# Running sums of squares on VectorE instead of GpSimd in a one-layer streaming encoder

## The chip, the cores and the metric

The kernel runs on one core of one Trainium2 chip. A core has five engines with instruction queues of their own, each worked off in order: TensorE (PE in the profile, its weight loads PEld), VectorE (DVE), ScalarE (ACT), GpSimd (POOL) and SyncE (SP, which here issues DMAs). They meet through semaphores. The metric is the device time of one execution in microseconds (us), the median of several runs.

## The reference

One layer of an encoder is applied to two groups of rows with the same weights: 1024 prompt rows and 32 sample rows of width 1024. Cut to what matters here:

```python
def rms_norm(x, g):
    y = xf * lax.rsqrt(jnp.mean(xf * xf, axis=-1, keepdims=True) + EPS)
    return (y * g.astype(jnp.float32)).astype(x.dtype)

h = rms_norm(x, g_mix)
z = h @ w_in                     # q, k, v, conv, gates
a = attn_core(q, k, v) @ w_attn_out
bo = (cb * conv) @ w_conv_out
x = x + (jax.nn.sigmoid(ga) * a + jax.nn.sigmoid(gb) * bo) @ w_mix_out      # "mixed" rows
hc = rms_norm(x, g_cross)
x = x + co @ w_co                # co: attention of hc @ w_cq into 256 memory tokens; "crossed" rows
hm = rms_norm(x, g_mlp)
x = x + jnp.square(jax.nn.relu(hm @ w_up)) @ w_down                         # "last" rows
y = rms_norm(x, norm_final_g)
```

All is float32. Each `rms_norm` needs the mean of the squares of a row over its 1024 features.

## The kernel before, in words

The rows lie along the free axis of a tile and the features along the 128 partitions, so that x is 8 tiles (f = 0 to 7) for each of three chunks of rows (c = 0, 1, 2 with 384, 384 and 288 columns). A product in full precision is made of three matrix products on TensorE (`gemm`, L176 to L178; `do_co`, L1293 to L1295; `part`, L1706 to L1708): operands are split into a rounded high part (ScalarE, L120, or L150 for a kept weight) and a rest (VectorE, L121). A weight of 128x1024 is fetched by SyncE, split into `wh` and `wl`, and taken by TensorE up to three weights later.

The sum over features has two steps. Along f, the squares of the tiles are added up, column by column, into a piece of the tile `xacc`; this is `square_acc`. For f = 0 the square is written straight into `xacc`, for f > 0 into a temporary tile `ct` and then added. Then `stats_col` (L207) lets TensorE add up the 128 partitions into `pq`, and VectorE and ScalarE make the factor 1/sqrt (L209 to L215), which `stats_row` spreads over a tile R (L223 to L226). `ct` has six buffers, used in turn by many steps; a buffer is free again when its last reader is done.

`square_acc` is called in three stages, for each chunk:
- `do_mix` (mixed rows): VectorE adds the product in the accumulator to the row (L1154, into a tile of `Ga` or `Gb`), `gain_split` splits it for the next product (L256 on ScalarE, L257 on VectorE), and the square of f = 0 to 6 is made by GpSimd (L249), that of f = 7 by ScalarE (L251).
- `do_co` (crossed rows): TensorE makes the products of two tiles f side by side in two of the three accumulators; VectorE adds each to the row (L1298), ScalarE squares it (L251).
- `to_x1` with `squares_of` (last rows): VectorE adds the last product (L1696), ScalarE squares it (L251). For chunk 2 the last square is not added; `last_row` gives it to TensorE as a second operand (L1752).

Chunk c's cross attention stands beside chunk c+1's mixing in the program (`beside`), so that crossed rows of one chunk and mixed rows of the next share a stretch of time. GpSimd also adds in `do_conv_out` (L1140), squares in `up_part` (L1356), and makes sums of weights (L881 to L884); a kernel-wide scheduler fixes the order of instructions in each queue from durations that it assumes, except for those pinned by hand. At the end `final` and `final_last` scale the rows and store them (L1741, L1788, L1790).

Of the kernel before, what the change touches and what calls it, by code (L numbers as in the profile page):

```python
# [13 lines left out]
ALU = mybir.AluOpType  # L14
# [24 lines left out]
def hybrid_step(ctx: ExitStack, tc: tile.TileContext, io):  # L39
    nc = tc.nc  # L40
    act, dve, pool_e, pe, sp = nc.scalar, nc.vector, nc.gpsimd, nc.tensor, nc.sync
# [54 lines left out]
    def tmp(n, dt=F32):  # L96
        return tp.tile([P, n], dt, tag="ct", bufs=NCT, name=nm("ct"))
# [144 lines left out]
    def square_acc(x, f, c, on_pool=False):  # L242
        n = CH[c][1]
        if f == 0:
            accs[c] = [xacc[0][:, CH[c][0] : CH[c][0] + n]]
        acc = accs[c][0]
        sq = tmp(n) if f else acc
        if on_pool:
            pool_e.tensor_tensor(sq, x, x, op=ALU.mult)  # L249
        else:  # L250
            act.activation(sq, x, AF.Square)  # L251
        if f:
            pool_e.tensor_tensor(acc, acc, sq, op=ALU.add)  # L253

    def scaled_split(hi, lo, x, g):
        act.mul(hi, x, col(g))  # L256
# [889 lines left out]
    def do_mix(c, f):  # L1146
        def fn(w):
            n = CH[c][1]
            xt = cr.tile([P, n], F32, tag="xt", bufs=3, name=nm("xt"))
            sp.dma_start(xt, io[f"x{c}"][:, f])  # L1150
            a = acc_tile([P, n])
            gemm(a, w, mg[c])
            x = gate_slot(c, f)
            dve.tensor_add(x, a, xt)  # L1154
            x1[c][f] = x
            xc[c][f] = gain_split(x, G_CROSS + f, c)
            square_acc(x, f, c, on_pool=f < NF - 1)

        return fn
# [122 lines left out]
    def do_co(c, half):  # L1282
        def fn(w):
            n = CH[c][1]
            wh, wl = w
            fs = range(4 * half, 4 * half + 4)
            for f in fs:
                if f % 2 == 0:
                    two = [acc_tile([P, n]) for _ in range(2)]
                    for k, g in ((k, g) for k in range(2) for g in range(2)):  # L1290
                        s = slice((((f + g) % 4) * 2 + k) * P, (((f + g) % 4) * 2 + k) * P + P)
                        hi, lo = co[c][k]
                        pe.matmul(two[g], wh[:, s], hi, start=(k == 0), stop=False)  # L1293
                        pe.matmul(two[g], wh[:, s], lo, start=False, stop=False)
                        pe.matmul(two[g], wl[:, s], hi, start=False, stop=(k == 1))  # L1295
                a = two[f % 2]
                x = x1[c][f]
                dve.tensor_add(x, a, x)  # L1298
                if half == 0 and c == 2:
                    xm[c][f] = gain_split(x, G_MLP + f, c)  # L1300
                square_acc(x, f, c)
            if half == 1 and c == 2:
                for f in fs:
                    xm[c][f] = gain_split(x1[c][f], G_MLP + f, c)

        return fn
# [377 lines left out]
    def squares_of(c, x):  # L1684

        if c == 2 and done[c] == NF - 1:
            sq = tmp(CH[c][1])
            act.activation(sq, x, AF.Square)
            accs[c].append(sq)
        else:  # L1690
            square_acc(x, done[c], c)
        done[c] += 1
# [283 lines left out]
```

## Time and profile before

| | |
|---|---|
| median of 3 runs | 1769.81 us (1769.12 to 1770.55) |
| the profiled execution's own time | 1767.74 us |
| its span (first to last instruction) | 1766.0 us |
| granted TensorE clock, mean | 0.997 |
| busy: PE, DVE, ACT, POOL | 1733.7, 1213.3, 846.1, 657.9 us |
| the adds of `square_acc` (L253) | 62 on POOL, 78.0 us |

Rows of the profile name an engine, a line of the kernel (L253), the tile written and those read (`xacc<-xacc,ct`), and partitions x elements. A group row has the busy time in us and the mean of one in ns, then the idle time of the engine just before, with what ended it. A timeline row has its start and its length in us, and in brackets the idle time before it. In a row of a chain there are a start, a length, and what ran.

### The profile page before, as it was taken

How to read it: one execution, taken by the hardware profiler on the slowest of the kernel's cores; microseconds unless marked ns; L12 is line 12 of the kernel's file. 1: busy time of each engine (PE TensorE's matmuls, PEld its weight loads, DVE VectorE, ACT ScalarE, POOL GpSimd, SP SyncE). 2: the span in 40 equal slices, each digit the busy share in tenths (PEclk: the TensorE clock that was granted, in tenths of full speed). 3: DMA queues.
4: the chain of work that ended last, by engine and by line, in shares of the span. 5: the costliest groups of instructions: out<-in, count | busy, mean ns of one | idle time of the engine just before them, and what ended most of it. 6: DMA issues, size and time to landing. Idle time of an engine off the chain costs nothing.

```text
span 1766.0 us, 30039 instructions
## 1 busy us (share of the span) xinstructions
PE 1733.7 (98%) x11008; PEld 1711.6 (97%) x11008; DVE 1213.3 (69%) x2130; ACT 846.1 (48%) x1625; POOL 657.9 (37%) x702
## 2 busy tenths in 40 slices
PE   8999999999999999999999999999999999999997
PEld 8999999999999999999999999999999999999997
DVE  6768888777887767367576877666666675445665
ACT  8667767852232245144465755642222353432553
POOL 2246675643744534402324241375544300100111
PEclk9999999999999999999999999999999999999998
DMA  5413434442322527789766767744443497544674
GB/s 183 146 58 106 141 114 147 139 153 98 132 86 96 177 102 263 261 255 320 259 218 208 242 219 240 253 166 155 130 139 124 149 316 221 176 152 141 230 240 134
DMA packets 178115, 313.01 MB, mean 177 GB/s; under 512 B 18192, under 2 KB 137776, under 8 KB 177840
## 3 DMA queue, kind: packets, MB, share of 16 engines
q1 hardware_dynamic: 168320, 276.97, 47.2%
q0 software_dynamic: 9216, 33.56, 5.4%
q8 instruction: 86, 1.41, 0.3%
q10 hardware_dynamic: 432, 0.58, 0.1%
q14 instruction: 61, 0.50, 0.1%
HBM read 233.23 MB, written 77.81 MB: 176 GB/s over the span
## 4 chain that ended last, share of the span: by engine, by line
PE 72%; DMA 9%; DVE 6%; ACT 5%; issue 3%; POOL 2%; SPq 1%; POOLq 0%; DVEq 0%; ACTq 0%
PE acc L176 7%; PE acc L178 7%; PE acc L177 7%; PE acc L892 7%; PE acc L894 7%; PE acc L893 7%; PE acc L1707 5%; PE acc L1706 5%; PE acc L1708 5%; PE pa L177 3%; PE pa L178 3%; PE pa L176 3%; DVE wl L121 2%; ACT wh L120 1%; PE pt L589 1%
## 5 line engine op out<-in xcount | busy, mean ns | idle before, releaser
L120 ACT CAST wh<-wr 128x1024 fp32r<-128x1024 f32 (+1 forms) x224 | 234.1, 1045 | 311.4 <-PE acc L1707 77.1
L121 DVE TENSOR_TENSOR wl<-wr,wh 128x1024 fp32r<-128x1024 f32 (+1 forms) x224 | 307.3, 1372 | 93.2 <-ACT wh L120 91.7
L176 PE MATMUL acc<-Y,wh 128*128 128x384 f32 (+1 forms) x624 | 201.9, 324 | 2.6 <-DVE ct L1081 1.5
L178 PE MATMUL acc<-Y,wl 128*128 128x384 f32 (+1 forms) x624 | 201.6, 323 | 0.3 <-DVE wl L121 0.3
L177 PE MATMUL acc<-Y,wh 128*128 128x384 f32 (+1 forms) x624 | 201.6, 324 | 0.0
L253 POOL TENSOR_TENSOR xacc<-xacc,ct 128x384 f32<-128x384 f32 (+1 forms) x62 | 78.0, 1257 | 322.2 <-ACT ct L251 319.8
L176 PE MATMUL acc<-X,wh 128*128 128x384 f32 (+1 forms) x528 | 172.6, 327 | 1.2 <-ACT wh L120 1.2
L177 PE MATMUL acc<-X,wh 128*128 128x384 f32 (+1 forms) x528 | 171.8, 325 | 0.9 <-DVE X L257 0.9
L178 PE MATMUL acc<-X,wl 128*128 128x384 f32 (+1 forms) x528 | 171.0, 324 | 0.0
L176 PEld LDWEIGHTS acc<-Y,wh 128*128 128x128 f32 x624 | 117.0, 188 | 3.9 <-DVE ct L1081 1.9
L178 PEld LDWEIGHTS acc<-Y,wl 128*128 128x128 f32 x624 | 117.2, 188 | 0.6 <-DVE wl L121 0.6
L177 PEld LDWEIGHTS acc<-Y,wh 128*128 128x128 f32 x624 | 117.1, 188 | 0.0
L579 POOL TENSOR_SCALAR S<-S,rec 128x256 f32<-128x256 f32 (+1 forms) x96 | 93.3, 984 | 62.1 <-DVE rec L576 61.9
L1706 PE MATMUL acc<-Y,wh 128*128 128x384 f32 (+1 forms) x352 | 113.1, 321 | 0.2 <-ACT Y L120 0.2
L1707 PE MATMUL acc<-Y,wh 128*128 128x384 f32 (+1 forms) x352 | 113.1, 321 | 0.1
L1708 PE MATMUL acc<-Y,wl 128*128 128x384 f32 (+1 forms) x352 | 112.9, 321 | 0.0
L120 ACT CAST wh<-s 128x1024 fp32r<-128x1024 f32 x54 | 56.6, 1051 | 105.9 <-PE acc L893 72.3
L177 PEld LDWEIGHTS acc<-X,wh 128*128 128x128 f32 x528 | 100.0, 189 | 2.9 <-DVE X L257 1.8
L176 PEld LDWEIGHTS acc<-X,wh 128*128 128x128 f32 x528 | 99.8, 189 | 2.2 <-ACT wh L120 1.4
L178 PEld LDWEIGHTS acc<-X,wl 128*128 128x128 f32 x528 | 99.8, 189 | 1.0 <-DVE wl L121 0.2
L121 DVE TENSOR_TENSOR Y<-ct,Y 128x384 fp32r<-128x384 f32 (+1 forms) x128 | 68.9, 570 | 28.7 <-ACT Y L120 28.5
L120 ACT CAST Y<-ct 128x384 fp32r<-128x384 f32 (+1 forms) x128 | 59.2, 486 | 60.0 <-DMA ct<-bc_d 14.8
(405 smaller groups left out, 5360.3 us busy)
## 6 DMA issues: line engine op xcount, KB each, us to landing
wr<-in_w_in SPq DMA_DIRECT2D x55, 512.0 KB, 3.6
wr<-in_w_up SPq DMA_DIRECT2D x48, 512.0 KB, 3.8
wr<-in_w_down SPq DMA_DIRECT2D x32, 512.0 KB, 4.0
wr<-wsum_d SPq DMA_DIRECT2D x32, 512.0 KB, 3.5
wl<-wl_d SPq DMA_DIRECT2D x28, 512.0 KB, 4.8
wr<-in_w_conv_out SPq DMA_DIRECT2D x24, 512.0 KB, 4.5
wr<-in_w_mix SPq DMA_DIRECT2D x24, 512.0 KB, 4.7
xacc<-in_w_down POOLq DMA_DIRECT2D x21, 512.0 KB, 3.9
```

The lines of the kernel that those rows point to most:

```text
L120: act.copy(hi, src)
L121: dve.tensor_sub(lo, src, hi.bitcast(F32))
L176: pe.matmul(out, wh[:, a], hi, start=(k == 0), stop=False)
L177: pe.matmul(out, wh[:, a], lo, start=False, stop=False)
L178: pe.matmul(out, wl[:, a], hi, start=False, stop=(k == len(acts) - 1))
L579: pool_e.tensor_scalar_mul(stl[:, h, :nk], stl[:, h, :nk], rec[:, h : h + 1])
L892: pe.matmul(acc, wh[:, a], hi, start=(start and k == 0), stop=False, skip_group_check=True)
L893: pe.matmul(acc, wh[:, a], lo, start=False, stop=False, skip_group_check=True)
L894: pe.matmul(acc, wl[:, a], hi, start=False, stop=(k == 3), skip_group_check=True)
L1706: pe.matmul(a, wh[:, s], hi, start=(start and k == 0), stop=False, skip_group_check=True)
L1707: pe.matmul(a, wh[:, s], lo, start=False, stop=False, skip_group_check=True)
L1708: pe.matmul(a, wl[:, s], hi, start=False, stop=(stop and k == len(acts) - 1), skip_group_check=True)
```

## The change

The add of a square to the running sum is issued on VectorE's queue instead of GpSimd's. It is the same sum of the same operands. The squares stay where they were made: on GpSimd for f = 0 to 6 of the mixed rows, on ScalarE otherwise. It touches 62 adds: 7 for each chunk of the mixed rows, 7 for each chunk of the crossed rows, and 7, 7 and 6 of the last rows.

```diff
@@ -250,7 +250,7 @@
         else:
             act.activation(sq, x, AF.Square)
         if f:
-            pool_e.tensor_tensor(acc, acc, sq, op=ALU.add)
+            dve.tensor_add(acc, acc, sq)
 
     def scaled_split(hi, lo, x, g):
         act.mul(hi, x, col(g))
```

## The prediction

> **What bounds the kernel now.** I read the page from the top: busy times, the chain that ended last, and the group that the change rewrites.
>
> ```profile
> span 1766.0 us, 30039 instructions
> PE 1733.7 (98%) x11008; PEld 1711.6 (97%) x11008; DVE 1213.3 (69%) x2130; ACT 846.1 (48%) x1625; POOL 657.9 (37%) x702
> PE 72%; DMA 9%; DVE 6%; ACT 5%; issue 3%; POOL 2%; SPq 1%; POOLq 0%; DVEq 0%; ACTq 0%
> L253 POOL TENSOR_TENSOR xacc<-xacc,ct 128x384 f32<-128x384 f32 (+1 forms) x62 | 78.0, 1257 | 322.2 <-ACT ct L251 319.8
> ```
>
> PE is busy for 1733.7 of 1766.0 us. Its matrix products are untouched, so the change can only act on the 32.3 us in which PE is idle. The adds themselves are POOL's 78.0 us, 62 of them at 1257 ns, on an engine that is busy 37% of the time. Who waits for them is asked of the line itself, and where PE is idle is read by stage (the columns that matter are the stretch, its length, then the busy times of PE, PEld, DVE, ACT and POOL).
>
> ```profile
> L253 POOL TENSOR_TENSOR xacc<-xacc,ct x62: 802/1127/2137, 833.8 to 1749.5; 128x384 f32<-128x384 f32 x42, 128x288 f32<-128x288 f32 x20
>   ACT ct L251: 319.8, 31
> who waited for it (us, times):
> ...
> 830.00:935.00 105.00, 105.00 (x623) 104.70 (x622) 69.72 (x113) 56.51 (x100) 35.42 (x31) 1.00 0.69 234
> 935.00:1065.00 130.00, 124.21 (x824) 120.49 (x823) 94.70 (x178) 78.89 (x150) 46.91 (x44) 1.00 0.69 232
> 1065.00:1135.00 70.00, 68.15 (x434) 67.09 (x433) 51.98 (x103) 42.45 (x94) 19.79 (x20) 1.00 0.70 240
> 1495.00:1735.00 240.00, 240.00 (x1478) 239.85 (x1478) 134.90 (x204) 103.61 (x172) 23.58 (x18) 1.00 0.56 183
> 1735.00:1766.00 31.00, 22.03 (x155) 20.78 (x153) 16.03 (x37) 8.66 (x17) 4.81 (x5) 0.84 0.37 126
> ```
>
> Nobody waited for an add: the list under "who waited for it" is empty. So the sums being ready earlier is worth nothing. The adds lie in two places: 42 between 830 and 1135 us (mixed and crossed rows), 20 from 1495 us on (last rows). In the second place PE is busy for 240.00 of 240.00 us until the tail. What can move is in the first: PE idles 0 us in 830 to 935, 5.79 us in 935 to 1065 and 1.85 us in 1065 to 1135, 7.64 us in all. The waits of PE there (engine, tile and line, whom it waited for, us in total, times, longest), from 830 to 1125 us and, the last row, from 1110 to 1200:
>
> ```profile
> PE acc L1293 <- DVE Gb L1298: 1.9, 2, 1.3
> PE acc L1293 <- DVE Ga L1298: 1.5, 2, 1.4
> PE acc L176 <- ACT M L120: 1.2, 1, 1.2
> ...
> PE acc L1293 <- DVE Gb L1298: 0.7, 1, 0.7
> ```
>
> The largest are the cross output products (L1293) that wait until VectorE has read an earlier product out of its accumulator (L1298). VectorE, the engine that gets the adds, is what PE waits for. That is where the sum is made.
>
> **The change part by part.** *Removed from POOL:* 62 adds. Nothing waited for POOL's result, so the direct gain is 0. What may gain is VectorE, which runs slower beside such an add. The first place, of one stretch in order of time:
>
> ```profile
> 942.73 0.83 POOL L249 TENSOR_TENSOR ct<-Gb 128x384 f32<-128x384 f32 x1 [1.00 <-DVE Gb L1154]
> 943.64 1.86 POOL L253 TENSOR_TENSOR xacc<-xacc,ct 128x384 f32<-128x384 f32 x1
> ...
> 943.05 1.59 DVE L121 TENSOR_TENSOR wl<-wr,wh 128x1024 fp32r<-128x1024 f32 x1 [0.40 <-ACT wh L120]
> 944.56 1.35 DVE L257 SCALAR_TENSOR_TENSOR Y<-Gb,prm,Y 128x384 fp32r<-128x384 f32 x1
> ...
> 946.44 0.44 PE L1293 MATMUL acc<-Y,wh 128*128 128x384 f32 x1 [1.26 <-DVE Gb L1298]
> ...
> 841.89 1.23 DVE L121 TENSOR_TENSOR wl<-wr,wh 128x1024 fp32r<-128x1024 f32 x1 [2.07 <-ACT wh L120]
> 857.39 0.62 DVE L257 SCALAR_TENSOR_TENSOR Y<-Gb,prm,Y 128x384 fp32r<-128x384 f32 x1 [2.92 <-ACT Y L256]
> 855.74 1.01 POOL L253 TENSOR_TENSOR xacc<-xacc,ct 128x384 f32<-128x384 f32 x1
> ```
>
> The weight split L121 takes 1.23 us with POOL still and 1.59 beside the square and the add; the row split L257 takes 0.62 and 1.35. Both are ahead of the L1298 that PE waits 1.26 us for. Without the add they are shorter by 0.36 + 0.73 = 1.09 us, and PE's wait falls to about 0.17. The second place is alike, at the smaller shape:
>
> ```profile
> 1033.31 1.07 POOL L253 TENSOR_TENSOR xacc<-xacc,ct 128x288 f32<-128x288 f32 x1 [0.96 <-ACT ct L251]
> 1033.63 1.06 DVE L257 SCALAR_TENSOR_TENSOR Y<-Gb,prm,Y 128x288 fp32r<-128x288 f32 x1
> 1035.22 0.44 PE L1293 MATMUL acc<-Y,wh 128*128 128x384 f32 x1 [0.61 <-DVE Gb L1298]
> 1121.71 0.51 DVE L257 SCALAR_TENSOR_TENSOR Y<-Gb,prm,Y 128x288 fp32r<-128x288 f32 x1
> ```
>
> L257 at 1.06 instead of 0.51 gives 0.55 us of the 0.61 back. I take these two, 1.09 + 0.55 = 1.64 us, as the whole gain; the upper bound is all 7.64 us of idle time in the stage.
>
> *Added to DVE:* 62 adds of two SBUF operands. The same operation on the same shapes already runs there:
>
> ```profile
> L1140 DVE TENSOR_TENSOR sgl<-sgl,ct 128x384 f32<-128x384 f32 x2 | 1.1, 554 | 0.0
> L1140 DVE TENSOR_TENSOR sgl<-sgl,ct 128x288 f32<-128x288 f32 x1 | 0.4, 440 | 0.0
> ```
>
> Of the 42 adds of the first place 28 have 384 columns and 14 have 288: 28 x 0.55 + 14 x 0.44 = 21.6 us. In 830 to 1135 VectorE is busy for 69.72 + 94.70 + 51.98 = 216.4 of 305 us; with the adds at most 238.0, 78%, before the relief is taken off. It stays far from being the bound on average. In the last rows it is 14 x 0.55 + 6 x 0.44 = 10.3 us on 134.90 of 240, which PE's products cover; if that cover were gone, 10.3 us is what it would cost.
>
> So the cost is not the load but the place in VectorE's queue. An add can stand ahead of an L1298 that PE waits for. There are five such places, the five waits for L1298 in the rows above (1.9, 1.5 and 0.7 us in sum): two in the first chunk, two in the second, one in the third. The first two chunks have 384 columns, the third 288: 4 x 0.55 + 0.44 = 2.64 us if one add stands in front each time, 0 if none does. An add becomes ready only when ScalarE has made the square of the row that L1298 has just written, so the next read-out may well come first; the rows don't tell which order it will be. I take half, 1.32 us, and keep 0 and 2.64 for the range.
>
> *The waits that it adds.* On POOL the adds waited 319.8 us for squares, with nothing queued behind them. On VectorE what stands behind a waiting add is: the weight splits L121 (PE waits for them), the read-outs L1154 and L1298 (free an accumulator), L257, L1321 and L1325 (rows of the next products). The 18 mixed squares made by POOL (L249) were ahead of their adds in one queue; now VectorE waits for them across engines. SP's queue gets no DMA more and no fewer, but its loads of t1 share the six temporary buffers with the squares, and a buffer comes free when its add is done. I put these waits at 0, because a VectorE instruction can be ordered ahead of an add that is not ready; the next part prices the other case.
>
> *The tail.* Does the end come earlier or later?
>
> ```profile
> 1748.40 0.44 DVE L1696 TENSOR_TENSOR Gb<-acc,Gb 128x288 f32<-128x288 f32 x1
> 1749.51 0.80 POOL L253 TENSOR_TENSOR xacc<-xacc,ct 128x288 f32<-128x288 f32 x1 [1.45 <-ACT ct L251]
> 1753.42 0.46 DVE L1696 TENSOR_TENSOR Gb<-acc,Gb 128x288 f32<-128x288 f32 x1 [4.57 <-PE acc L1708]
> 1753.22 0.73 PE L1752 MATMUL pq<-ones,xacc 128*128 128x1 f32 x6
> ```
>
> The last add ends at 1750.31, the column sums that read it start at 1753.22, behind PE's last products: 2.91 us of slack, and VectorE is idle for 4.57 us there. An add of 0.44 us fits. The last square of the last chunk is not added at all. The tail costs 0 and gains 0.
>
> *The sum.* -1.64 + 1.32 = -0.3 us on the profiled execution, which took 1767.74 us (1766.0 us of span and 1.74 around it). The median of the runs is 1769.81, 2.07 above it; on that I forecast 1769.5 us.
>
> [...] When the add at 943.64 ran beside VectorE's two-operand instructions it took 1.86 us instead of 1.01, and they grew too. [...]
>
> **The rivals.** *Slower: the add blocks VectorE's queue.* ScalarE makes the squares, and a weight copy may be in front of one:
>
> ```profile
> 936.97 0.17 PE acc L1294
> ...
> 938.04 1.04 ACT L150 CAST wh<-wr 128x1024 fp32r<-128x1024 f32 x1
> 946.48 1.46 ACT L251 ACTIVATE ct<-Gb 128x384 f32<-128x384 f32 x3 [2.95 <-DVE Gb L1298]
> ```
>
> If VectorE's order puts an add right behind its row and a copy of 1.04 us is in front of the square, the read-out behind the add is late by 1.04 + 0.55 us. At five places: 5 x 1.04 + 2.64 - 1.64 = +6.2, 1776.0 us. It decides from the point where VectorE is late by more than the three products, 0.17 us each by the row above, that PE still has in hand when the first of two accumulators is to be read out. For it: POOL waited 31 times. Against it: squares come in threes behind the read-outs (the 946.48 row), so a read-out was ahead of them. Chance 0.22.
>
> [...] Each add in front also meets a square of POOL (0.83 us, the 942.73 row): half of 5 x 0.83 + 2.64, 3.4, less 1.64, +1.8: 1771.6 us. For it: the grown rows. Against it: 21 of the 42 adds, the crossed ones, have their squares from ScalarE, and where these run POOL has less left to do. Chance 0.15.
>
> *Faster: more of the idle time goes.* If relief on VectorE shortens half of the 7.64 us, the gain is 3.8: 1766.0 us. For it: both named waits stand behind instructions that an add had slowed. Against it: the wait for M L120 (1.2 us) hangs on a load and not on an add. Chance 0.15.
>
> *Nothing moves* (an equal trade, or adds hidden throughout) ends at 1769.8, within the forecast's own range. That the change doesn't do its work is excluded: 62 instructions change engine.
>
> **How the numbers follow.** A measurement of this kernel can tell about 0.2%, 3.5 us, from no change. Forecast -0.3 with its own bounds (-1.64 to +1.0): 0.48, all within 0.2%. The ports: 0.15. The blocked queue: 0.22, slower. More idle time gone: 0.15, of which 0.13 beyond the 3.5 us, since its price is just over that, and 0.02 within. Of the ports' 0.15 I count 0.02 as slower: with a square met at all five places it costs 4.15 + 2.64 - 1.64 = 5.2 us. That gives 0.13 faster, 0.48 + 0.13 + 0.02 = 0.63 within, 0.24 slower. The likeliest case's own range is 1768.2 to 1770.8. Eight times in ten asks for the two outer cases: low 1765.5, just under the faster rival, and high 1776.0, the blocked queue.
>
> **What would show it.** Right: 62 VectorE adds of some 0.55 and 0.44 us, no POOL instruction on that line; L121 near 1.23 and L257 near 0.62 before the L1293 products; PE's waits for L1298 in sum within 1 us of 3.4; PE full in 1495 to 1735; the last add over 2 us ahead of the column sums. Wrong: VectorE idle before adds with ScalarE or POOL as the releaser, PE waits on L121 or L1298 grown to several us, new idle time of PE in 830 to 935 or after 1135, where the change has no step, from instructions that moved in the queues.

## The result, and the profile after

The changed kernel takes 1778.01 us (median of 5 runs, 1776.82 to 1779.84), the kernel before 1769.81 us (5 runs, 1766.81 to 1772.05). The ratio is 1.0055, with a 95% interval of 1.0044 to 1.0066: 8 to 9 us slower, where I forecast no change. The profiled execution took 1776.82 us. Two lines of its page, and then what the trace has on the line of the adds:

```profile
span 1775.0 us, 30000 instructions
PE 1737.9 (98%) x11008; PEld 1715.0 (97%) x11008; DVE 1227.3 (69%) x2192; ACT 845.3 (48%) x1625; POOL 579.9 (33%) x640
```

```profile
L253 DVE TENSOR_TENSOR xacc<-xacc,ct x62: 440/549/922, 837.0 to 1759.5; 128x384 f32<-128x384 f32 x42, 128x288 f32<-128x288 f32 x20
  ACT ct L251: 2.9, 6
who waited for it (us, times):
```

The adds did what was expected of them: 0.55 and 0.44 us each, VectorE idle for only 2.9 us in front of them, and nobody waiting for one. The loss is elsewhere. The next fences are busy times by stretch (length, then PE, PEld, DVE, ACT, POOL, then PEclk, DMA share, GB/s), before and then after:

```profile
935.00:1069.00 134.00, 128.21 (x848) 124.49 (x847) 98.55 (x186) 80.70 (x153) 47.58 (x45) 1.00 0.69 230
1069.00:1139.00 70.00, 68.15 (x439) 67.09 (x439) 49.56 (x101) 42.29 (x95) 19.21 (x20) 1.00 0.71 244
1139.00:1200.00 61.00, 58.86 (x390) 57.96 (x390) 45.18 (x56) 25.88 (x42) 38.85 (x30) 1.00 0.56 189
1430.00:1500.00 70.00, 68.89 (x441) 67.73 (x440) 47.57 (x88) 30.49 (x57) 0.00 (x0) 1.00 0.81 261
```

```profile
935.00:1069.00 134.00, 126.39 (x827) 123.23 (x826) 100.94 (x203) 79.31 (x151) 19.93 (x20) 0.97 0.66 223
1069.00:1139.00 70.00, 68.09 (x433) 67.05 (x433) 53.18 (x107) 41.51 (x92) 12.22 (x13) 1.00 0.74 246
1139.00:1200.00 61.00, 57.57 (x378) 55.39 (x377) 39.01 (x55) 27.32 (x47) 35.02 (x28) 1.00 0.51 173
1430.00:1500.00 70.00, 66.16 (x426) 65.08 (x426) 47.46 (x90) 29.02 (x57) 0.00 (x0) 1.00 0.85 275
```

PE's idle time (length less PE) goes from 5.79 to 7.61 us in the first row, from 1.85 to 1.91 in the second, from 2.14 to 3.43 in the third and from 1.11 to 3.84 in the last: 5.9 us more. (Over the whole span it is 4.8 us more, 37.1 against 32.3: in the first 20 us PE shows 1.3 us less idle time, with no more products done by 40 us.) Two of these rows, with 4.0 of the 5.9 us, hold no add at all: the adds stand in 830 to 1135 us and after 1495 us. And the first row has a second new thing, a clock of 0.97 where it was 1.00. The longest new wait is there. The timeline around it (start, length, and in brackets the idle time before and its releaser), ScalarE before and then, of after, also the VectorE and PE rows at its two ends:

```profile
1021.92 0.51 ACT L1274 CAST Y<-tO 64x384 fp32r<-64x384 f32 x1 [2.05 <-DVE tO L1268]
1022.45 0.51 ACT L1279 CAST h<-tO 64x384 fp32r<-64x384 f32 x1
...
1026.30 1.04 ACT L150 CAST wh<-wr 128x1024 fp32r<-128x1024 f32 x1 [0.57 <-DMA wr<-in_w_co]
```

```profile
1024.13 0.54 DVE L1268 TENSOR_TENSOR tO<-o,tO 64x384 f32<-64x384 f32 x1
...
1025.84 1.04 ACT L150 CAST wh<-wr 128x1024 fp32r<-128x1024 f32 x1 [2.27 <-DMA wr<-in_w_co]
1026.90 0.51 ACT L1274 CAST Y<-tO 64x384 fp32r<-64x384 f32 x1
1027.44 0.51 ACT L1279 CAST h<-tO 64x384 fp32r<-64x384 f32 x1
...
1027.47 1.33 PE L1293 MATMUL acc<-Y,wh 128*128 128x384 f32 x3 [3.73 <-ACT Y L1274]
```

The same three ScalarE instructions stand in another order. L1274's operand was there at 1024.67 (VectorE's L1268), but in front of it a weight copy waited 2.27 us for its transfer, and PE waited 3.73 us for Y. What held Y here is that copy, which the diff doesn't touch. (A moved add, 0.92 us long, stands right ahead of L1268 in VectorE's queue, at 1023.29; the copy held Y for longer than the add did.) Behind the wait the clock falls; the stretches of after (the clock is third from the end), and two rows of PE's timeline:

```profile
1024.00:1027.00 3.00, 0.00 (x0) 0.00 (x0) 1.47 (x4) 1.14 (x2) 0.00 (x0) 0.82 0.80 311
1027.00:1030.00 3.00, 2.53 (x7) 2.23 (x8) 0.92 (x2) 0.93 (x2) 0.00 (x0) 0.50 0.57 188
1030.00:1034.00 4.00, 4.00 (x19) 4.00 (x19) 2.99 (x7) 3.06 (x5) 0.00 (x0) 0.65 0.00 0
```

```profile
1030.04 0.52 PE L1294 MATMUL acc<-Y,wh 128*128 128x384 f32 x1
1030.36 0.52 PE L1295 MATMUL acc<-Y,wl 128*128 128x384 f32 x1
```

These products start every 0.32 us; in the kernel before, the same kind started every 0.17:

```profile
1027.44 0.34 PE L1295 MATMUL acc<-Y,wl 128*128 128x384 f32 x1
1027.61 0.34 PE L1293 MATMUL acc<-Y,wh 128*128 128x384 f32 x1
```

While PE was busy this cost 0.50 x 2.53 + 0.35 x 4.00 = 2.7 us. So 5.9 us of waits and 2.7 us of slow products in these four stretches make 8.6 us, beside the 9.0 us between the spans. The last place is of the first kind again, in VectorE's queue (before, and then after with the PE row behind it):

```profile
1472.16 0.56 DVE L1542 TENSOR_TENSOR fold<-fold,fold 128x384 f32<-128x384 f32 x1 [4.49 <-DMA fold<-b_d]
1472.64 1.22 DVE L121 TENSOR_TENSOR wl<-wr,wh 128x1024 fp32r<-128x1024 f32 x1
```

```profile
1479.16 0.56 DVE L1542 TENSOR_TENSOR fold<-fold,fold 128x384 f32<-128x384 f32 x1 [4.87 <-DMA fold<-b_d]
1479.63 0.55 DVE L1696 TENSOR_TENSOR Ga<-acc,Ga 128x384 f32<-128x384 f32 x1
...
1481.49 1.74 DVE L1542 TENSOR_TENSOR fold<-fold,fold 128x384 f32<-128x384 f32 x3
1483.15 1.22 DVE L121 TENSOR_TENSOR wl<-wr,wh 128x1024 fp32r<-128x1024 f32 x1
...
1484.42 0.44 PE L1708 MATMUL acc<-H,wl 128*128 128x384 f32 x1 [2.10 <-DVE wl L121]
```

A weight split (L121) stands behind a subtraction (L1542) that waits 4.87 us for a transfer. Before, the split stood directly behind that subtraction; now seven instructions are between them.

Compared queue by queue, the two programs hold the same instructions, semaphores aside, but the scheduler ordered them differently, nearly always between about 925 and 1500 us, in a few places near 1750 us: apart from the adds, 704 positions differ on PE, 137 on VectorE, 94 on ScalarE, 66 on SyncE and 10 on GpSimd. So there were two changes in one, an engine and an order, and the experiments take them apart.

### The profile page after: what moved, and what is told of

Its sections match the earlier page's. It is cut to its first block, busy times and chain, and to the rows that moved or that the text cites. A ratio compares the mean times of both kernels' runs of the same rounds, so it can differ in the third digit from the quotient of the medians.

```text
span 1775.0 us, 30000 instructions
## 1 busy us (share of the span) xinstructions
PE 1737.9 (98%) x11008; PEld 1715.0 (97%) x11008; DVE 1227.3 (69%) x2192; ACT 845.3 (48%) x1625; POOL 579.9 (33%) x640
## 4 chain that ended last, share of the span: by engine, by line
PE 73%; DMA 9%; DVE 7%; ACT 5%; issue 4%; POOL 2%; SPq 1%; POOLq 0%; DVEq 0%; ACTq 0%
PE acc L176 8%; PE acc L177 7%; PE acc L178 7%; PE acc L892 7%; PE acc L894 7%; PE acc L893 7%; PE acc L1708 5%; PE acc L1706 5%; PE acc L1707 5%; PE pa L177 3%; PE pa L178 3%; PE pa L176 3%; DVE wl L121 2%; ACT wh L120 1%; DMA ct<-bc_d 1%
## 5 line engine op out<-in xcount | busy, mean ns | idle before, releaser
L121 DVE TENSOR_TENSOR wl<-wr,wh 128x1024 fp32r<-128x1024 f32 (+1 forms) x224 | 305.5, 1364 | 89.0 <-ACT wh L120 87.6
L1708 PE MATMUL acc<-Y,wl 128*128 128x384 f32 (+1 forms) x352 | 112.9, 321 | 0.0
L121 DVE TENSOR_TENSOR Y<-ct,Y 128x384 fp32r<-128x384 f32 (+1 forms) x128 | 67.8, 561 | 26.0 <-ACT Y L120 24.7
L749 POOL TENSOR_TENSOR xacc<-xacc 128x256 f32<-128x256 f32 x84 | 76.7, 913 | 27.3 <-DMA xacc<-in_w_down 23.2
```

The costliest lines, as they stand in the source:

```text
L121: dve.tensor_sub(lo, src, hi.bitcast(F32))
L1708: pe.matmul(a, wl[:, s], hi, start=False, stop=(stop and k == len(acts) - 1), skip_group_check=True)
```

## The experiments

**The order and the adds, each alone.** Theory: the new order costs the time and the adds don't. Rival: the adds block VectorE's queue, as in my own rival of 1776.0 us. From the first difference on, the order of every queue was written into the kernel as edges that only order and wait for nothing (written out for the kernel before itself, this gives its program unchanged). The by-hand pins of `normed_split` (L1321, L1325) are replaced by these edges. The diff is shortened: the list of orders and the names in it are packed in the kernel.

```diff
-            pool_e.tensor_tensor(acc, acc, sq, op=ALU.add)
+            dve.tensor_add(acc, acc, sq)
...
+    for names in orders_of_the_kernel_before:
+        for p, n in zip(names, names[1:]):
+            tc.add_manual_dep(made[n], p, no_sync, reason="order")
```

order_before:

> All 62 adds on VectorE, but every queue in the order that it had in the kernel before, written out as issue-order edges; each add stands in VectorE's queue where GpSimd had it in that order. Theory A (the time goes through the order in which the other instructions are issued, not through the adds): 1768 to 1772 us, within 0.2% of before, and no new wait of PE over 1 us near 1027, 1185 and 1480 us. Theory B (the adds themselves, their length and their waits for squares, hold up VectorE): 1775 to 1781 us, as the changed kernel.

It took 1765.91 us against 1768.99 for the kernel before on the same chip, ratio 0.9985 (0.9975 to 0.9996); repeated on another chip, 1766.18 against 1768.89:

> The kernel of order_before once more: all 62 adds on VectorE, every queue in the order of the kernel before. If its gain is the adds' own, the ratio to the kernel before lies again within 0.9975 to 0.9996; if the first look was an accident of the runs, it is 1.000 or above.

0.9985 again (0.9976 to 0.9995). In the order of before, the adds on VectorE make the kernel faster. The opposite corner, the adds left on GpSimd and all queues in the changed kernel's order:

> The adds stay on GpSimd as before; every queue has the order of the changed kernel. Theory A: 1775 to 1781 us, with PE's waits of the changed kernel at 1027 (3.7 us) and 1480 us. Theory B: 1767 to 1772 us, as before.

1779.30 us, ratio 1.0060 (1.0046 to 1.0074): the whole loss without the edit. In its trace PE waits 3.15 us for Y of L1274 at 1026.77 us, and the clock falls behind that wait as in the changed kernel:

```profile
1027.00:1030.00 3.00, 3.00 (x10) 2.70 (x11) 1.54 (x3) 0.72 (x2) 0.00 (x0) 0.50 0.67 274
```

ScalarE's queue is held by a weight copy here too, but by an earlier one (in_w_mix), which waits 3.20 us for its transfer until 1022.70 us. In a table, ratios to the kernel before:

| | order of before | order of after |
|---|---|---|
| adds on GpSimd | 1 | 1.0060 |
| adds on VectorE | 0.9985 | 1.0055 |

The order costs 0.6 to 0.7%. The adds gain 0.15% in the order of before, seen twice; the 0.05% in the other order lies well within the intervals. The rival fell. Where order_before gains, in the same stretches as above and in its timeline:

```profile
935.00:1069.00 134.00, 131.40 (x868) 127.83 (x867) 107.60 (x213) 82.45 (x156) 19.42 (x21) 1.00 0.70 233
1139.00:1200.00 61.00, 58.49 (x386) 57.65 (x386) 44.68 (x57) 24.45 (x40) 39.33 (x31) 1.00 0.54 183
1430.00:1500.00 70.00, 68.28 (x440) 67.47 (x439) 48.11 (x88) 31.07 (x57) 0.00 (x0) 1.00 0.79 258
```

```profile
944.44 1.65 DVE L121 TENSOR_TENSOR wl<-wr,wh 128x1024 fp32r<-128x1024 f32 x1 [0.40 <-ACT wh L120]
946.01 0.60 DVE L257 SCALAR_TENSOR_TENSOR Y<-Gb,prm,Y 128x384 fp32r<-128x384 f32 x1
...
947.14 0.44 PE L1293 MATMUL acc<-Y,wh 128*128 128x384 f32 x1 [0.58 <-DVE Gb L1298]
```

Idle time in 935 to 1069 us falls from 5.79 to 2.60 us, and 0.4 + 0.6 us of it are given back in the two later rows.

**Part of the adds.** Each with the scheduler left free.

```diff
-            pool_e.tensor_tensor(acc, acc, sq, op=ALU.add)
+            (dve if stage in moved else pool_e).tensor_tensor(acc, acc, sq, op=ALU.add)
```

mixed_only (21 adds):

> Only the 21 adds of the mixed rows go to VectorE, the scheduler orders freely. Theory B: about 21/62 to half of the 8.2 us, 1772.6 to 1774 us, and with the crossed ones alone it sums up to the whole. Theory A: depends on the order that comes out, between -2 and +8 us, and the parts need not add up.

crossed_only (21 adds):

> Only the 21 adds of the crossed rows go to VectorE, the scheduler orders freely. Theory B: 1772.6 to 1774 us, and mixed and crossed together make the 8.2 us. Theory A: between -2 and +8 us, and the two parts need not add up to 8.2 us.

last_only (the last rows' adds):

> Only the last rows' adds (18 of the 62) on VectorE, the scheduler left free; its order then differs from the kernel before in a few places alone (4 on VectorE, 4 on ScalarE, 20 on TensorE). Theory (the issue order is what costs, and the adds themselves do not): within 0.2% of the kernel before, 1767 to 1771 us. Rival (adds on VectorE cost in proportion to their number, 18 of 62 of the 8.2 us lost): about 1771.4 us.

Ratios 1.0027 (1.0016 to 1.0037), 1.0038 (1.0024 to 1.0053) and 1.0007 (0.9998 to 1.0016). The first two are reordered too, and lose 0.3 to 0.4%; their times, 1773.62 and 1774.62 us, lie in or close to the ranges of both theories and don't decide between them. The third keeps nearly the old order and is level, but its interval holds its rival's loss as well (2.4 of 1769 us, 1.0014). Its number, 18, in the expectation is a slip: the last rows have 20 adds.

**Which part of the order.** The changed kernel's order on all queues up to the first L1375 (about 1141 us) and that of before from there on, and the mirror image, both with all adds on VectorE.

> All 62 adds on VectorE. Every queue stands in the changed kernel's order up to the first combination of the cross stage's two heads (about 1141 us), from there in the order of the kernel before. With the order of the kernel before throughout, this program took 1765.9 us, with the changed order throughout about 1778: 12 us of order. Theory (the order loses time at three separate places): TensorE's progress in the changed kernel's trace is behind by +3.9 us at 1050, where the program in the old order was ahead by 3.4 us (from -1.75 less the +1.67 that it had before the first difference), so the first place holds about 6 to 7 us and this kernel takes 1771 to 1773 us. Rival (a delay in the middle is caught up where later work waits for transfers anyway, and only the last places count): 1766 to 1768 us.

> The mirror image: all 62 adds on VectorE, every queue in the order of the kernel before up to about 1141 us, and in the changed kernel's order from there. No add stands between 1135 and 1495 us. Theory (three separate places): the steps of +2.5 us near 1155 to 1185 and of +2.7 us near 1430 to 1485 remain, and with 1765.9 us for the old order throughout this gives 1770.5 to 1772 us. Rival (the later steps are only consequences of being late at 1141 us): 1766 to 1767 us.

1771.75 us, ratio 1.0031 (1.0017 to 1.0044), and 1769.01 us, ratio 1.0011 (1.0003 to 1.0020), on a chip where the kernel before took 1767.02 us. Against 0.9985 with the old order throughout, the first part of the order costs 0.46% and the second 0.26%, in sum 0.72; the whole costs 1.0055 - 0.9985 = 0.70. So the two parts add up within the intervals, and both rivals fell: the first part alone costs time, and so does the second. The split is not clean, though. In the trace of the first run (1775.11 us) TensorE also waits 3.02 us at 1172.19 us, past the seam of the two orders; the changed kernel waited 1.07 us there (1169.59); part of the 0.46% may belong to the seam.

**One instruction moved.** The changed kernel in its own order, but for ScalarE's weight copy shown above.

```diff
  ScalarE's queue at 1023 to 1028 us
-  L150 (w_co) , L1274 (Y) , L1279 (h)
+  L1274 (Y) , L1279 (h) , L150 (w_co)
```

> The changed kernel with its own issue order on every queue, but for one instruction: ScalarE's copy of the high part of a w_co tile (L150), which stands at about 1026 us ahead of the copy Y (L1274) and of h (L1279) and made ScalarE wait 2.27 us for the weight's transfer, is moved behind those two. Theory (this wait holds the cross stage's norm and with it TensorE, which waited 3.7 us for Y at 1027 us): 1.5 to 2.5 us less than the changed kernel, about 1775.5 to 1776.5 us. Rival (the norm would be late by VectorE's own queue, or the product that needs the weight waits in its place): no change, 1778 us.

1773.16 us, ratio 1.0039 (1.0026 to 1.0052), 0.16% or 2.8 us less than the changed kernel's 1.0055, if with intervals that overlap (1.0044 to 1.0052). In its trace PE waits 1.23 us there instead of 3.73, and the clock stays at 1.00 at this place:

```profile
1023.68 0.79 PE L1293 MATMUL acc<-Y,wh 128*128 128x384 f32 x3 [1.23 <-ACT Y L1274]
```

Two things in this trace keep the step from being a clean price of the copy. The clock falls at another place instead, behind a wait of 2.11 us at 1478.49 us: it is 0.89 over 1460 to 1490 us, and from 1478.97 us on the products start every 0.32 us. And an add has a part in the 1.23 us that are left: it ran for 0.92 us from 1021.70, right ahead of the L1268 (1022.54) on which Y now hangs, and L1268's operand was there at 1021.73. By these rows the add makes Y some 0.8 us later (an estimate). The list "who waited for it" does not show such a thing: in the changed kernel's trace it is empty for L253, although there, too, L1268 starts (1024.13) where an add ends (0.92 us from 1023.29).

**A second instruction moved.** On top of that, VectorE's weight split of 1483 us ahead of the fold subtraction that waits; and the same kind of move in the old order.

```diff
  VectorE's queue at 1473 to 1478 us
-  L1542 (waits) , L1696 x4 , L1542 x3 , L121 (wl)
+  L121 (wl) , L1542 (waits) , L1696 x4 , L1542 x3
```

> The run weight_copy_later (1773.2 us) with one more instruction moved: VectorE's subtraction that forms a wl tile of the stage after the cross stage (L121), at 1477.2 us, whose operands were ready at 1465.5 us, is put ahead of the fold subtraction (L1542) that stood before it and waited 5.44 us for its transfer, and so ahead of the four L1696 sums as well. Theory (the third place of the loss is this one instruction standing behind a wait for a transfer): TensorE's wait of 2.11 us at 1478.5 us goes, 1771 us, 0.1% less than weight_copy_later. Rival (the time is given back further on, as part of the gain of weight_copy_later was): 1773 us.

> The kernel of order_before with two wl subtractions (L121) of the stage after the cross stage put ahead of the fold subtractions (L1542) that wait for transfers there, at 1461 and 1471 us. In order_before TensorE waited 1.45 us for wl at 1473.1 us. Theory (an early operand behind a late one on VectorE's queue is what TensorE pays for): 1.2 to 1.5 us less than order_before, about 1764.5 us. Rival (another operand of that product comes just as late, or the fold's products are late in its place): the same as order_before, 1766 us.

two_moved took 1773.51 us, ratio 1.0034 (1.0022 to 1.0047); old_order_wl_first 1763.41 us, ratio 0.9981 (0.9968 to 0.9994). Against 1.0039 and 0.9985 neither step can be told from none by its time. The traces show why little is left: the wait for wl goes from 2.11 us to nothing in the first and from 1.46 us to nothing in the second, and the next operand in the same place is late instead, in two_moved L1696, which still stands behind the waiting subtraction, in old_order_wl_first a copy of ScalarE (one row of each):

```profile
1479.67 0.41 PE L1706 MATMUL acc<-H,wh 128*128 128x384 f32 x1 [1.23 <-DVE Ga L1696]
```

```profile
1479.95 0.40 PE L1706 MATMUL acc<-Y,wh 128*128 128x288 f32 x1 [1.18 <-ACT Y L120]
```

old_order_wl_first and order_before are the two versions that beat both kernels.

**Wait or clock.** What of the 3.73 us place is the wait, and what the clock behind it? Theory: the wait itself drops the clock. TensorE is given 16 repeats of a product inside the wait, which change no result and make nothing ready earlier.

```diff
+                        if (c, half, f, k, g) == (1, 0, 2, 0, 0):
+                            for _ in range(16):
+                                pe.matmul(two[g], wh[:, s], hi, start=True, stop=True)
                         pe.matmul(two[g], wh[:, s], hi, start=(k == 0), stop=False)
```

> The changed kernel in its own issue order, with 16 extra products on TensorE: the first product (L1293) of the third accumulator of that cross output stage is done 16 times more just before it is done for good, so that TensorE works through some 2.7 us (16 x 0.17) of the 3.74 us in which it waited for Y at 1023.7 to 1027.5 us. The results are overwritten and nothing gets ready earlier. Theory (TensorE's clock falls to half behind a long wait, which in the changed kernel's trace makes the products from 1027 to 1032.6 us come every 0.32 us instead of every 0.17): the granted clock stays at 1.00 there, and the kernel takes 2 to 2.7 us less than the changed kernel although it computes more, about 1775.5 us. Rival (the slow products have another cause, such as the transfers or VectorE beside them): the clock falls all the same and the time stays at 1778 us, or grows.

> The changed kernel itself, beside kept_busy on the same chip: 1778 us, ratio 1.0044 to 1.0066 as before. Where its trace shows a wait of TensorE of 1.5 us or more between 930 and 1500 us, theory (the clock) expects stretches at half the clock right behind some of these waits and nowhere else; rival: the stretches lie anywhere.

On one chip the changed kernel took 1777.51 us (1775.34 to 1779.06; ratio 1.0050, 1.0036 to 1.0064) and kept_busy 1775.11 us (1774.00 to 1777.14; ratio 1.0036, 1.0023 to 1.0048): 2.4 us less with more to compute, as the theory had it. The intervals overlap, but the clock separates them: a mean of 0.997 or 0.998 in each of the five runs of kept_busy and 0.995 or 0.996 in each of the other five. The repeats in the timeline of kept_busy (L1295 is the added line there; what stood at L1293 before is its L1296), its stretches, and after them those of after_again behind its waits of 2.50 us at 1023.90 and of 2.12 us at 1481.21:

```profile
1025.73 3.06 PE L1295 MATMUL acc<-Y,wh 128*128 128x384 f32 x16
```

```profile
1023.00:1027.00 4.00, 3.96 (x24) 3.36 (x23) 4.00 (x9) 2.51 (x4) 1.69 (x2) 1.00 0.75 254
1027.00:1030.00 3.00, 2.95 (x17) 2.46 (x15) 1.37 (x4) 2.08 (x3) 0.00 (x0) 1.00 0.85 292
1030.00:1034.00 4.00, 3.66 (x22) 3.25 (x22) 3.16 (x7) 2.27 (x4) 0.00 (x0) 1.00 0.41 141
```

```profile
1023.00:1027.00 4.00, 3.10 (x9) 2.79 (x10) 1.52 (x4) 1.68 (x4) 0.00 (x0) 0.61 0.77 286
1480.00:1484.00 4.00, 2.79 (x9) 2.79 (x10) 4.00 (x9) 0.00 (x0) 0.00 (x0) 0.66 0.76 240
1484.00:1488.00 4.00, 4.00 (x25) 4.00 (x24) 2.80 (x7) 2.56 (x6) 0.00 (x0) 0.92 1.04 328
```

Between 900 and 1500 us the traces of this case hold six waits of 2.5 us or more, and the clock fell with each: 3.73 us in the changed kernel and 3.15 in order_after (0.50 in 1027 to 1030 us in both), 3.5 in mixed_only (0.50 in 1028 to 1030), 2.9 and 3.0 in after_then_before (0.55 in 1030 to 1032, and 0.97 over 1140 to 1200), 2.50 in after_again (0.50 in 1024 to 1026). Where such a wait was filled, it stayed at 1.00. The trace of kept_busy also has a wait that was not filled, 2.3 us for wl (L1711), and the mean clock of that execution is 0.998 all the same. A shorter wait can leave the clock alone: in the changed kernel's trace it is 1.00 in 1484 to 1488 us, behind a wait of 2.10.

## Why the prediction was wrong

*The step that failed* is the one on the waits that the change adds: "I put these waits at 0, because a VectorE instruction can be ordered ahead of an add that is not ready". True of the adds, which VectorE hardly waited for (2.9 us in 62). (That GpSimd had nothing queued behind its adds was not quite so: in the kernel before, the square of 854.84 us stands right behind the add of 853.67.) But I priced only instructions around the adds, and took every other queue to stay as it was. The document's own description says that a kernel-wide scheduler orders each queue from assumed durations; an instruction with another engine and another assumed length is a new input for all queues. Two other statements of the prediction failed with it. "What can move is in the first" place (830 to 1135 us): 4.0 of the 5.9 us of new idle time lie in 1139 to 1200 and 1430 to 1500 us. And "the change can only act on the 32.3 us in which PE is idle": 2.7 us of the loss are products at half the clock, in which PE is busy. The term was mis-sized by the whole result: 0 by the prediction, 0.6 to 0.7% or 11 to 12 us by the table above. The sign was written down under "Wrong" (idle time "after 1135 ... from instructions that moved in the queues"), but as a warning, without a rival and a price. An order that can change needs both.

*The gain, -1.64 us*, was right in kind, and in size as far as the runs can tell: order_before is 2.7 us faster (0.15% of 1769; 0.7 to 4.4 us by its interval). At 946 us L257 fell from 1.35 to 0.60 us as predicted, but L121 did not: 1.65 us against 1.59, with no add on GpSimd, only the square (0.83 us from 944.18). So the 0.36 us that I put down to the add there did not go with it, and PE's wait went from 1.26 to 0.58 us instead of 0.17. The wait of 0.61 us at 1035 us went, as said. What I hadn't priced: at 1027 us PE's wait fell from 1.37 to 0.50 us in order_before.

*The cost of adds ahead of read-outs, +1.32 us*, was too much in the old order. At 947.01 us an add does stand between two L1298, and PE does not wait for the second. The net of the fixed order is a gain, so this term can't have been large there, but no run measures it alone. In the changed order an add does stand ahead of what PE waits for, at another instruction than I thought of: L1268, by some 0.8 us in weight_copy_later.

*The last rows and the tail* were right: PE is busy for 240.00 of 240.00 us in 1500 to 1740, and the last add ends at about 1760.0 us, 2.5 us ahead of the column sums (1762.5).

*The rivals.* The blocked queue, 1776.0 us, comes nearest in time and is wrong in kind: VectorE does not wait for squares, and with the order held there is no loss. Its number was a coincidence. The little slower one, 1771.6 us ("the ports" in the prediction's chances), fell too. No run shows its term, a whole square of GpSimd (0.83 us) for each add in front, or any ports: by the same two runs the moved adds cost nothing net beside GpSimd's work, and at most single rows are longer, such as the longest add of 0.92 us (at 1023.29, beside two squares of GpSimd) against 0.44 for the one of the same shape at 1021.25. The faster rival, 1766.0 us (0.9979 of before), comes near what order_before measures (0.9985): of the 7.64 us of idle time 3.1 go.

*What stays open.* Why the scheduler chose the order it chose was not tried; the moves of single instructions explain most of the 1027 us place and show what follows at 1480 us, while that of 1139 to 1200 us (1.3 us of idle time) was narrowed down only to the order of its stretch. Nor is it known why the clock fell to 0.66 (1480 to 1484 us) with a wait of 2.12 us in one execution of the changed kernel and stayed at 1.00 with one of 2.10 us in the same place of another.

## What to carry to other kernels

Where a scheduler orders the queues, moving an instruction to another engine is two changes, and the second may be the larger: compare the queues of both programs before reading anything into the time, and hold the order fixed to see what the edit itself does. In a changed order, look for instructions that wait for a transfer ahead of ones whose operands are ready; moving a single such weight copy took off about 2.8 us here. An empty list of waiters doesn't say that an instruction costs nothing: look at what stands behind it in its own queue. And a wait of TensorE can cost more than its length: with one of 3.73 us the clock fell to 0.50 here, and 2.7 us of slow products came on top.

## What the hardware showed beside this

A wait of TensorE is paid for twice when its clock falls. Besides the six waits of 2.5 us or more, shorter ones had a fall behind them: 2.12 us in after_again (0.66 in 1480 to 1484 us), 2.11 in weight_copy_later (0.89 over 1460 to 1490); in two_moved it stands behind 0.66 us of idle time in 1022 to 1024 and 1.21 in 1024 to 1026 (0.58 and 0.56 in 1026 to 1030). What a fall takes off, summed as the missing share of the clock over the stretches of such a place, idle time included, was 1.7 us or twice that where it was summed: 1.7 us in two_moved, mixed_only, after_then_before and after_again near 1022 to 1032, in after_again 0.34 x 4 + 0.08 x 4 = 1.7 us more at 1480 to 1488, in the changed kernel 0.18 x 3 + 0.50 x 3 + 0.35 x 4 = 3.4 us at 1024 to 1034, where the clock is 0.50 from 1026.0 to 1032.7. The length of the wait alone does not decide: the 2.10 us wait at 1484.42 us in the first trace of the changed kernel left the clock at 1.00, the 2.12 us wait in the same place of after_again did not, and before_then_after with a wait of 2.0 us for wl (L1708) and kept_busy with one of 2.3 us have a mean clock of 0.998, as high as any execution here. What else decides was not shown.
